# Local attention units at fixed places, turning transfers on two queues, and a later weight split

## The chip, the cores and the metric

One core of one Trainium2 chip runs the kernel. The metric is the device time of one execution in microseconds (us), the median of several runs. TensorE (PE) multiplies; ScalarE (ACT) and VectorE (DVE) work on what it leaves in its accumulators (PSUM banks); GpSimd (POOL) clears tiles and issues transfers; SyncE (SP) only issues transfers (DMA).

## What is computed

Two layers of an encoder over 512 tokens of width 1024. Layer 0 mixes tokens by attention in three head groups (dilations 1, 4 and 16), layer 1 by a gated linear attention. After each mixer comes a SwiGLU.

```python
for g, (window, dilation) in enumerate(((128, 1), (512, 4), (2048, 16))):
    q = rope(rms_norm(qkv[:, :, g, 0], q_gain[g]), positions)
    k = rope(rms_norm(qkv[:, :, g, 1], k_gain[g]), positions)
    o, lse = dilated_window_attention(q, k, qkv[:, :, g, 2], window, dilation)
    outs.append(o); lses.append(lse)
alpha = jax.nn.softmax(jnp.stack(lses, axis=0), axis=0)
out = jnp.sum(alpha[..., None] * jnp.stack(outs, axis=0), axis=0)
h = h + out.reshape(bsz, seq, A_WIDTH) @ w_out
h = h + (jax.nn.silu(g) * u) @ w_down      # g, u = split(rms_norm(h) @ w_gate_up)
```

## The kernel before

Every float32 weight of 128x1024 is split into a high part (`wh`, an ACT copy, L96) and a low part (`wl`, a DVE subtraction, L97), and every product is three matmuls: high by high, low by high, high by low. Weights are loaded through SP's queue (L103), two ahead.

**Attention.** Layer 0 comes in two stages. In each, the work goes by four units u of four heads.

- `attend_dilated(u)` (dilations 4 and 16) projects k, v and q of the unit (`qk_chunk`, `v_chunk`), then computes scores (L777, L782), softmax, transposes and the weighted sum of values. Results go through DRAM (`o_dram`, `st_dram`) by POOL's queue (L765, L793).
- `attend_local(u)` (dilation 1) computes scores (L816) with q and k from `qk_chunk("qk", u)`, the softmax over four pairs of blocks, the transposes (L683), the weighted sum (L723), transposes back (L744), and merges the three groups (`combine`).

A chunk (`chunk_of`, L592 to L594) is 96 matmuls of 128x512 into four PSUM banks (tag "pp", of which there are four), so the next chunk's first matmul waits until ACT has copied the bank out (L614, `zs<-ppp`). After a q or k chunk, ACT and DVE normalize and rotate; DVE transposes blocks of 32 (L636); then **the turning**: 16 transfers of 64 KB (L640, `zq<-zs` or `zs<-zs`), all on SP's queue, carry the blocks to their places; and ACT copies them straight (L649, `zq<-zs` or `qk<-zq`), which the scores read.

**The softmax** (L670 to L675) of one group of scores is a DVE reduction with the mask, an exponential on ACT, and in local units two memsets on POOL of what the mask leaves out (`sm<-`, 64 columns). PE's transposes read the whole tile `sm`. The weighted sum of a group is issued after the next group's transposes (`pending`, `later`).

**The order.** A scheduler of the tile framework places instructions on each engine's queue; a program order, priorities (`high_priority`) and `issue_after` steer it. In `attention`, before, unit u of the local attention is written after the projection of unit u+1, and the scheduler spreads the softmax groups among the matmuls of the chunk that follows. `out_attention` (after the attention phase, called through `swiglu`) multiplies by the output weights in two parts: part 0 with the first half of the heads' outputs, part 1 with the second. `load_h` loads the residual (`h<-in_xT_dram`).

**Gate and up** (`gate_up`) runs six blocks j of columns through seven products each, fed by `forms`; the last block has 256 columns. Sums of weights are formed by transfers that add (POOL, L256). `copy` (L398) takes two accumulators into `g` on ACT. `forms.first` loads the next block's first weights into `wf` and splits them (`ready`) ahead of time.

## Time and profile before

| what | value |
|---|---|
| time, median of 3 runs | 1460.18 us (1459.81 to 1460.34) |
| the profiled execution | 1461.01 us, span 1459.2 us |
| granted TensorE clock, mean | 0.999 |
| local attention stage, from the span's start | about 380 to 545 us |
| last gate and up block of layer 0, of layer 1 | about 753 us, about 1310 us |

Rows of the timeline give the start in us from the span's start, the duration in us, engine, line and operation, output and input, a count where several are grouped, and in brackets the idle time of the engine before it and what released it. Matmuls are pipelined, so one row's duration is longer than the distance to the next. A row of the waits gives the engine, its instruction and what it waited for, with the total in us, the number of times and the longest.

### The profile page before, as it was taken

To read this page: it belongs to the slowest core of one execution; us is meant where nothing else is said; L and a number is where in the kernel's file an instruction comes from. 1 tells how busy PE (TensorE), PEld (TensorE's weight loads), DVE (VectorE), ACT (ScalarE), POOL (GpSimd) and SP (SyncE) were. 2 spreads that over 40 slices of the span, in tenths; PEclk is the share of its full clock that TensorE was granted. 3 is DMA by queue.
4 is the path that set the end of the run, shared out by engine and by line. 5 is a ranking of instruction groups with operands and counts; after the bars stand their busy time and mean duration, and the time that the engine had idled before them with its cause. 6 is when DMAs were issued, how large, how long until landed. Compare 5 with 4: busy or idle time off the path is not lost.

```text
span 1459.2 us, 21024 instructions
## 1 busy us (share of the span) xinstructions
PE 1441.3 (99%) x7742; PEld 1186.7 (81%) x7742; DVE 1012.9 (69%) x1824; ACT 752.6 (52%) x1291; POOL 149.0 (10%) x256
## 2 busy tenths in 40 slices
PE   8999999999999999999999999999999999999998
PEld 6887878787778878888888887888888888879887
DVE  6596867778577769977787334847576987779321
ACT  6344444545566746655566233556744755556221
POOL 0001020100100011122221000000010222221000
PEclk9999999999999999999999999999999999999999
DMA  8644343453533355788777333212156787778431
GB/s 276 180 141 107 102 115 119 109 173 101 136 88 88 104 156 157 215 228 231 231 209 217 98 101 97 89 58 80 52 155 192 214 218 221 217 186 251 144 105 62
DMA packets 99832, 219.62 MB, mean 151 GB/s; under 512 B 15216, under 2 KB 42416, under 8 KB 99728
## 3 DMA queue, kind: packets, MB, share of 16 engines
q1 hardware_dynamic: 83376, 166.74, 35.5%
q0 software_dynamic: 16352, 51.53, 16.1%
q8 instruction: 61, 1.00, 0.3%
q14 instruction: 43, 0.35, 0.1%
HBM read 185.64 MB, written 19.99 MB: 141 GB/s over the span
## 4 chain that ended last, share of the span: by engine, by line
PE 78%; DVE 11%; ACT 4%; DMA 3%; issue 2%; SPq 1%; DVEq 0%; ACTq 0%
PE ppp L110 18%; PE ppp L333 12%; PE ppp L112 9%; PE ppp L592 6%; PE ppp L593 6%; PE ppp L594 6%; PE ppp L338 6%; PE ps L333 4%; DVE wl L97 2%; PE ps L338 2%; PE po L723 2%; DMA wf<-in_gate_up_last_dram 1%; PE ps L683 1%; DVE zs L636 1%; DVE sq L635 1%
## 5 line engine op out<-in xcount | busy, mean ns | idle before, releaser
L97 DVE TENSOR_TENSOR wl<-wf,wh 128x1024 fp32r<-128x1024 f32 (+1 forms) x200 | 239.1, 1196 | 200.8 <-ACT wh L96 200.4
L96 ACT ACTIVATE wh<-wf 128x1024 fp32r<-128x1024 f32 (+1 forms) x200 | 208.4, 1042 | 316.4 <-PE ppp L110 172.7
L592 PE MATMUL ppp<-wh,xs 128*128 128x512 f32 (+1 forms) x672 | 258.5, 386 | 6.8 <-ACT wh L96 5.5
L593 PE MATMUL ppp<-wl,xs 128*128 128x512 f32 (+1 forms) x672 | 257.9, 384 | 0.1
L594 PE MATMUL ppp<-wh,xs 128*128 128x512 f32 (+1 forms) x672 | 257.4, 383 | 0.0
L110 PE MATMUL ppp<-xs,wh 128*128 128x512 f32 x544 | 170.3, 393 | 0.0
L592 PEld LDWEIGHTS ppp<-wh,xs 128*128 128x128 f32 x672 | 127.1, 189 | 35.8 <-ACT wh L96 5.5
L594 PEld LDWEIGHTS ppp<-wh,xs 128*128 128x128 f32 x672 | 127.2, 189 | 25.5 <-issue 1.2
L593 PEld LDWEIGHTS ppp<-wl,xs 128*128 128x128 f32 x672 | 127.2, 189 | 25.0 <-issue 1.1
L96 ACT ACTIVATE wh<-wA 128x1024 fp32r<-128x1024 f32 x88 | 93.4, 1061 | 104.4 <-PE ppp L333 39.5
L333 PE MATMUL ppp<-wh,a 128*128 128x512 f32 (+1 forms) x576 | 139.7, 373 | 1.7 <-ACT g L398 1.7
L97 DVE TENSOR_TENSOR wl<-wA,wh 128x1024 fp32r<-128x1024 f32 x88 | 107.1, 1217 | 20.1 <-ACT wh L96 20.1
L333 PEld LDWEIGHTS ppp<-wh,a 128*128 128x128 f32 x576 | 101.9, 188 | 23.1 <-ACT g L398 4.6
L110 PEld LDWEIGHTS ppp<-xs,wh 128*128 128x128 f32 x544 | 101.7, 188 | 22.5 <-issue 0.8
L112 PE MATMUL ppp<-xs,wl 128*128 128x512 f32 x272 | 106.1, 391 | 0.0
L671 ACT ACTIVATE sm<-sm,st 128x160 f32<-128x160 f32 (+2 forms) x128 | 56.8, 446 | 44.5 <-DVE st L670 44.4
L338 PE MATMUL ppp<-wl,a 128*128 128x512 f32 (+1 forms) x288 | 78.4, 371 | 0.0
L256 POOL DMA_DIRECT2D wA<-in_gate_up_dram x44 | 38.5, 875 | 323.0 <-DVE wl L97 250.9
L333 PE MATMUL ppp<-wh,sh 128*128 128x512 f32 (+1 forms) x192 | 70.3, 371 | 0.0
L333 PE MATMUL ppp<-wh,sl 128*128 128x512 f32 (+1 forms) x192 | 70.3, 371 | 0.0
L333 PE MATMUL ps<-wh,sh 128*128 128x512 f32 (+1 forms) x192 | 70.3, 371 | 0.0
L333 PE MATMUL ps<-wh,sl 128*128 128x512 f32 (+1 forms) x192 | 70.3, 371 | 0.0
(302 smaller groups left out, 2583.0 us busy)
## 6 DMA issues: line engine op xcount, KB each, us to landing
wA<-in_gate_up_dram POOLq DMA_DIRECT2D x52, 512.0 KB, 6.2
wf<-in_gate_up_dram SPq DMA_DIRECT2D x40, 512.0 KB, 5.0
wf<-in_down_dram SPq DMA_DIRECT2D x32, 512.0 KB, 3.7
wf<-in_a_w_v_dram SPq DMA_DIRECT2D x20, 512.0 KB, 3.8
turned<-g POOLq DMA_DIRECT2D x80, 128.0 KB, 7.3
wf<-in_a_w_q_dram SPq DMA_DIRECT2D x16, 512.0 KB, 3.8
zq<-zs SPq DMA_DIRECT2D x128, 64.0 KB, 2.1
wf<-in_a_w_qk_dram SPq DMA_DIRECT2D x16, 512.0 KB, 3.7
```

The source lines that it names most:

```text
L96: nc.scalar.activation(hi, src, AF.Copy)
L97: self.low = nc.vector.tensor_sub(lo, src, hi.bitcast(F32))
L110: mm(out, lhsT=wh, rhs=part, start=start and k + n == 0, stop=False)
L112: self.multiplied = mm(out, lhsT=wl, rhs=x[0], start=False, stop=stop and k == len(w) - 1)
L256: self.added = nc.gpsimd.dma_start(raw[tag][i], dram[block, i], accum_op=ALU.add)
L333: mm(acc[i][:, 0:width], lhsT=x_part[:, i * P:(i + 1) * P], rhs=wh[:, f], start=first, stop=False, skip_group_check=True)
L338: self.multiplied = mm(acc[i][:, 0:width], lhsT=x[k][0][:, i * P:(i + 1) * P], rhs=wl[:, f], start=False, stop=k == last, skip_group_check ...
L592: mm(a, lhsT=xh, rhs=wh[:, f], start=k == 0, stop=False)
L593: mm(a, lhsT=xh, rhs=wl[:, f], start=False, stop=False)
L594: self.multiplied = mm(a, lhsT=xl, rhs=wh[:, f], start=False, stop=k == KT - 1)
L671: nc.scalar.activation(sm[:, w], sm[:, w], AF.Exp, bias=n, scale=-1.0, accum_out=l)
L723: self.nc.tensor.matmul(o, lhsT=vals(i0 + b, c, c0 + a * HD), rhs=pts[a][b][c], start=c == 0, stop=c == 1)
```

## The change

Three things, and what they need.

1. **Turning on two queues.** Of the 16 transfers of each turning, those with a + b odd are issued by GpSimd instead of SP.
2. **Fixed places.** `attend_local` becomes a generator that stops after each softmax group. `chunk_of` and `project` count ticks, one for each block k of a chunk (12 matmuls of 128x512 or 128x256) or of a `project`, and at given ticks a visit runs the next part of a unit, behind the matmul just issued. The 16 visits are spread by hand over qk chunks 2 and 3, two value chunks and part 0 of the output projection, which moves into the attention phase as `out_part(0)`. `load_h` and the splits of the outputs come before it. In `softmax`, the memsets are written ahead of the reduction and the exponential.
3. **A later split.** In the last gate and up block, the splits of `first` are ordered after ACT's copy that was issued last (`issue_after(self.copied.ins)`).

The lines of the changed kernel have other numbers: L640 becomes L652, L614 L625, L616 L627, L649 L661, L670 to L675 L682 to L687, L683 L695, L701 L713, L723 L735, L738 L750, L816 L829, L96 L98, L398 L401.

**ACT, between the last scores of unit 0 and the chunk of unit 3.** `sm` are the exponentials, `pt` and `ob` copies of transposes and of the weighted sum, `zq` the straight copies of unit 1, `zs` the copies that free the chunk's banks. Before:

```order
L671 ACTIVATE sm_4119,st_695_4066<-sm_4119,st_695_4066 128x192
L835 ACTIVATE mw_4459<-mw_4459 128x16
L701 ACTIVATE pt_4163<-ps_4108 128x512
L701 ACTIVATE pt_4165<-ps_4107 128x512
L96 ACTIVATE wh_4664<-wf_4662 128x1024
L649 ACTIVATE zq_3970<-zs_3953 128x512 x4
L614 ACTIVATE zs_4291<-ppp_4167 128x512
L614 ACTIVATE zs_4291<-ppp_4168 128x512
L616 ACTIVATE wb_4294<-zs_4291 128x512
L616 ACTIVATE wb_4299<-zs_4291 128x512
```

And after the change:

```order
L687 ACTIVATE sm_4173,st_708_4160<-sm_4173,st_708_4160 128x256
L713 ACTIVATE pt_4221<-ps_4162 128x512
L713 ACTIVATE pt_4223<-ps_4161 128x512
L661 ACTIVATE zq_3970<-zs_3953 128x512 x4
L750 ACTIVATE ob_4219<-po_4145 128x512
L687 ACTIVATE sm_4231,st_708_4160<-sm_4231,st_708_4160 128x256
L687 ACTIVATE sm_4231,st_708_4160<-sm_4231,st_708_4160 128x192
L687 ACTIVATE sm_4237,st_708_4160<-sm_4237,st_708_4160 128x256
L687 ACTIVATE sm_4237,st_708_4160<-sm_4237,st_708_4160 128x192
L625 ACTIVATE zs_4249<-ppp_3998 128x512
L625 ACTIVATE zs_4249<-ppp_3999 128x512
```

The copies of `zq` were followed at once by those that free the banks (`zs`); now an `ob` and the four exponentials of unit 0's last group stand between them.

**ACT, the last gate and up block of layer 0.** `g_7438` are the two copies of accumulators, `wf` the loaded weights, `a` and `xs` other splits. Before:

```order
L398 ACTIVATE g_7438<-ppp_7195 128x512
L96 ACTIVATE wh_7506<-wf_7504 128x1024
L398 ACTIVATE g_7438<-ppp_7196 128x512
L96 ACTIVATE a_7441<-h_6627 128x512
L96 ACTIVATE xs_7445<-h_6670 128x512
L487 ACTIVATE wA_7773<-h_6716 128x512
L96 ACTIVATE wh_7550<-wf_7548 128x1024
```

And after the change:

```order
L401 ACTIVATE g_7438<-ppp_7195 128x512
L401 ACTIVATE g_7438<-ppp_7196 128x512
L98 ACTIVATE a_7441<-h_6627 128x512
L98 ACTIVATE xs_7445<-h_6670 128x512
L98 ACTIVATE wh_7506<-wf_7504 128x1024
L98 ACTIVATE wh_7550<-wf_7548 128x1024
```

The split of `wf_7504` stood between the two copies; now it stands behind them and behind two other splits, with the split of `wf_7548` next to it.

**POOL, the memsets of units 0 and 1.** `stn` and `on` are loads of what the dilated units left in DRAM. Before:

```order
L675 MEMSET sm_4113 128x64
L675 MEMSET sm_4119 128x64
L673 MEMSET sm_4387 128x64
L800 DMA stn_4928<-st_dram_2574 128x4x8
L803 DMA on_4378<-o_dram_0_1710 128x4x128
L673 MEMSET sm_4393 128x64
L675 MEMSET sm_4434 128x64
```

And after the change:

```order
L684 MEMSET sm_4083 128x64
L682 MEMSET sm_4167 128x64
L652 DMA zs_3953<-zs_3920 32x4x128 x8
L682 MEMSET sm_4173 128x64
L684 MEMSET sm_4231 128x64
L684 MEMSET sm_4237 128x64
L682 MEMSET sm_4421 128x64
L682 MEMSET sm_4427 128x64
```

Eight issues of the turning of unit 1 (`zs_3953`) now stand between two memsets of one softmax group of unit 0 (`sm_4167` and `sm_4173`).

On PE, the matmuls of a chunk between a group's scores and its transposes were 38, 33, 30, 13, 10, 38, 20, 10 and 10 in the first units; after the change they are 42, 32, 16, 21, 43 and 17 full-width ones in the first groups, 33 to 47 half-width ones in the value chunks, and 18 full-width ones in the output projection.

The diff, in full:

```diff
@@ -1,6 +1,7 @@
 import math
-from contextlib import ExitStack, contextmanager
+from contextlib import ExitStack, contextmanager, nullcontext
 from functools import partial
+from itertools import chain
 
 import numpy as np
 
@@ -47,6 +48,7 @@
         self.ps = ctx.enter_context(tc.tile_pool(name="ps", bufs=1, space=PSUM))
         self.dr = ctx.enter_context(tc.tile_pool(name="dr", bufs=1, space=DRAM))
         self.n = 0
+        self.visiting({})
 
     BASE = {"xs": 16, "h": 8, "wf": 2, "wh": 3, "wl": 3, "R": 1, "acc": 1, "sq": 1,
             "cols": 1, "ident": 1, "ones": 1, "eps": 1}
@@ -278,7 +280,8 @@
                 load(0, "wA")
                 return ready("wA")
             load(0, "wf")
-            return ready("wf")
+            with nullcontext() if ahead else self.tc.issue_after(self.copied.ins):
+                return ready("wf")
 
         def second():
             if own and not started:
@@ -575,7 +578,17 @@
             self.mm3(ps, [(wh[:, c], wl[:, c])], [self.x[k]], k == 0, k == KT - 1)
         return ps
 
-    def chunk_of(self, dram, lhs, width=S, ready=None, visit=None):
+    def tick(self):
+        self.ticks += 1
+        visit = self.visits.pop(self.ticks, None)
+        if visit:
+            with self.tc.issue_after(self.multiplied.ins):
+                visit()
+
+    def visiting(self, visits):
+        self.ticks, self.visits = 0, dict(visits)
+
+    def chunk_of(self, dram, lhs, width=S, ready=None):
         nc = self.nc
         acc = [self.p("pp") for _ in range(NT)]
         per = 1024 // width
@@ -592,9 +605,7 @@
                     mm(a, lhsT=xh, rhs=wh[:, f], start=k == 0, stop=False)
                     mm(a, lhsT=xh, rhs=wl[:, f], start=False, stop=False)
                     self.multiplied = mm(a, lhsT=xl, rhs=wh[:, f], start=False, stop=k == KT - 1)
-                if k == 1 and visit:
-                    with self.tc.issue_after(self.multiplied.ins):
-                        visit()
+                    self.tick()
         return acc
 
     def tokens(self, off):
@@ -637,8 +648,9 @@
         turned = self.t("zs" if kind == "qk" else "zq", (P, 4, 4, NT, 32))
         for a in range(4):
             for b in range(4):
-                nc.sync.dma_start(turned[32 * b:32 * b + 32, :, a].rearrange("p c i j -> p c (i j)"),
-                                  blocks[32 * a:32 * a + 32, :, b].rearrange("p c i j -> p c (i j)"))
+                queue = (nc.sync, nc.gpsimd)[(a + b) % 2]
+                queue.dma_start(turned[32 * b:32 * b + 32, :, a].rearrange("p c i j -> p c (i j)"),
+                                blocks[32 * a:32 * a + 32, :, b].rearrange("p c i j -> p c (i j)"))
         if kind == "k":
             return turned
         straight = []
@@ -666,13 +678,13 @@
         sm = self.t("sm")
         for b, (lo, hi) in enumerate(spans):
             w = slice(b * width + lo, b * width + hi)
-            n, l = stats[b]
-            nc.vector.tensor_tensor_reduce(sm[:, w], ps[:, w], mask[:, lo:hi], 1.0, 3e38, ALU.add, ALU.min, n)
-            nc.scalar.activation(sm[:, w], sm[:, w], AF.Exp, bias=n, scale=-1.0, accum_out=l)
             if lo > 0:
                 nc.gpsimd.memset(sm[:, b * width:b * width + lo], 0.0)
             if hi < width:
                 nc.gpsimd.memset(sm[:, b * width + hi:(b + 1) * width], 0.0)
+            n, l = stats[b]
+            nc.vector.tensor_tensor_reduce(sm[:, w], ps[:, w], mask[:, lo:hi], 1.0, 3e38, ALU.add, ALU.min, n)
+            nc.scalar.activation(sm[:, w], sm[:, w], AF.Exp, bias=n, scale=-1.0, accum_out=l)
         return sm
 
     def turned(self, pss, sms, count, width, finish):
@@ -794,8 +806,9 @@
                                 st[32 * r:32 * r + 32].rearrange("p a b c -> p (a b c)"))
         return o_dram, std
 
-    def attend_local(self, u, q, k, v, o_dram, std):
-        nc = self.nc
+    def attend_local(self, u, qk, v, o_dram, std):
+        nc = self.nc
+        q, k = qk[u]
         far = self.t("stn", (P, NT, 2, 4))
         nc.gpsimd.dma_start(far, std.rearrange("(j i a b) -> i j a b", i=P, a=2, b=4))
         for pr in range(2):
@@ -818,11 +831,13 @@
                 for a in range(2):
                     stats = [[st[:, s, i0 + b, a:a + 1] for s in range(2)] for b in range(2)]
                     sms.append(self.softmax(pss[a], spans, 256, self.masks[:, 160:416], stats))
+                yield
                 pts = self.turned(pss, sms, 4, P, self.finish_local)
                 c0 = (u if u < 2 else 0) * 256 + pr * P
-                vals = lambda i, c, f: v[(i + c) % 4][:, f:f + HD]
+                vals = lambda i, c, f: v[u][(i + c) % 4][:, f:f + HD]
                 then = partial(self.turn_back, partial(self.combine, u, pr, far, st, on)) if i0 == 2 else None
                 self.pending = pts, vals, c0, i0, then
+        yield
 
     def combine(self, u, pr, far, st, on, po):
         nc = self.nc
@@ -892,38 +907,48 @@
             v = [self.v_chunk(self.ins["a_w_v0"], 8)] * 2
             self.o = []
             self.inputs_read = False
-            for u in range(4):
-                if u < 3:
-                    qk.append(self.qk_chunk("qk", u + 1))
-                if u > 1:
-                    v.append(self.v_chunk(self.ins["a_w_v0b"][u - 2], 8, 256))
-                if u == 3:
-                    self.o = [self.split(e, (P, S), "xs", "xs") for e in self.o]
-                    self.inputs_read = True
-                self.attend_local(u, *qk[u], v[u], *far[u])
+            qk.append(self.qk_chunk("qk", 1))
+            units = chain.from_iterable(self.attend_local(u, qk, v, *far[u]) for u in range(4))
+            visit = partial(next, units, None)
+            both = lambda: (visit(), visit())
+            visit()
+            self.visiting({n: visit for n in (10, 24, 30)})
+            qk.append(self.qk_chunk("qk", 2))
+            self.visiting({n: visit for n in (4, 8, 20, 28)})
+            qk.append(self.qk_chunk("qk", 3))
+            self.visiting({4: visit, 16: both, 30: visit})
+            v.append(self.v_chunk(self.ins["a_w_v0b"][0], 8, 256))
+            self.visiting({n: visit for n in (12, 28)})
+            v.append(self.v_chunk(self.ins["a_w_v0b"][1], 8, 256))
+            self.load_h(self.ins["xT"], None)
+            self.o = [self.split(e, (P, S), "xs", "xs") for e in self.o]
+            self.inputs_read = True
+            self.visiting({4: both, 10: visit, 16: visit, 22: visit, 28: visit})
+            self.out_part(0)
+            for _ in units:
+                pass
             while self.pending or self.later:
                 self.run_later()
                 self.weigh_pending()
-            self.load_h(self.ins["xT"], None)
 
     def project(self, m, w, c0, xs):
         ps = self.p("pp")
         for k, x in enumerate(xs):
             c = slice((c0 + k) * P, (c0 + k + 1) * P)
             self.mm3(ps, [(w[0][:, c], w[1][:, c])], [x], k == 0, k == len(xs) - 1)
+            self.tick()
         self.nc.vector.tensor_add(self.h[m], ps, self.h[m])
 
-    def out_attention(self):
+    def out_part(self, part):
         half = KT // 2
-        for part in range(2):
-            for t in range(half):
-                w = self.weight(self.ins["a_w_out"][part, t], 1024)
-                for i, m in enumerate((half + t, t)):
-                    self.project(m, w, half * i, self.o[half * part:half * (part + 1)])
-                    if part:
-                        self.enter_blocks(m)
+        for t in range(half):
+            w = self.weight(self.ins["a_w_out"][part, t], 1024)
+            for i, m in enumerate((half + t, t)):
+                self.project(m, w, half * i, self.o[half * part:half * (part + 1)])
                 if part:
-                    self.pair_sums(t)
+                    self.enter_blocks(m)
+            if part:
+                self.pair_sums(t)
 
     def out_gla(self):
         for m in range(KT // 2):
@@ -988,7 +1013,8 @@
         o = [None] * 8
 
         def vals(half, visit):
-            acc = self.chunk_of(self.ins["b_w_v"][half], lambda kk, i: [x[:, i * P:(i + 1) * P] for x in self.x[kk]], visit=visit)
+            self.visiting({2 * NT: visit})
+            acc = self.chunk_of(self.ins["b_w_v"][half], lambda kk, i: [x[:, i * P:(i + 1) * P] for x in self.x[kk]])
             for i in range(NT):
                 vt = self.t("v")
                 ACT(vt, acc[i], AF.Copy, scale=Rc[:, i:i + 1])
@@ -1249,7 +1275,7 @@
             k.attention()
         if "ffn0" in phases:
             assert "attn" in phases
-            k.swiglu(0, 8 if "gla" in phases else None, k.out_attention)
+            k.swiglu(0, 8 if "gla" in phases else None, partial(k.out_part, 1))
         if "gla" in phases:
             if "ffn0" not in phases:
                 k.load_h(ins["xT"], 8)
```

## The prediction

> **What bounds the kernel now.** I read the page first. TensorE (PE) is busy for nearly the whole span, and no other engine comes close.
>
> ```profile
> span 1459.2 us, 21024 instructions
> PE 1441.3 (99%) x7742; PEld 1186.7 (81%) x7742; DVE 1012.9 (69%) x1824; ACT 752.6 (52%) x1291; POOL 149.0 (10%) x256
> ```
>
> So only time in which TensorE stands still can be won. The view of the waits, for PE over the whole span, gives us in total, times, and the longest. The first row is the kernel's start, which the change leaves alone.
>
> ```profile
> PE ppp L592 <- ACT wh L96: 5.5, 1, 5.5
> PE ps L816 <- ACT zq L649: 2.7, 1, 2.7
> PE ppp L333 <- ACT g L398: 1.7, 2, 0.9
> PE ps L683 <- ACT sm L671: 1.3, 5, 0.3
> PE ppp L592 <- ACT zs L614: 1.3, 3, 0.7
> ```
>
> The second row is the largest that the change can touch. Its place, in PE's timeline:
>
> ```profile
> 422.33 0.40 PE L594 MATMUL ppp<-wh,xs 128*128 128x512 f32 x1
> 425.44 1.06 PE L816 MATMUL ps<-zq 64*128 64x192 f32 x8 [2.71 <-ACT zq L649]
> 426.44 0.79 PE L592 MATMUL ppp<-wh,xs 128*128 128x512 f32 x1
> ...
> 429.59 0.47 PE L593 MATMUL ppp<-wl,xs 128*128 128x512 f32 x1
> 429.89 0.40 PE L594 MATMUL ppp<-wh,xs 128*128 128x512 f32 x1
> ```
>
> Matmuls shown as 0.39 us start 0.22 to 0.23 us apart; I count 0.227. The scores of unit 1 could have started at 422.33 + 0.23 = 422.56; they start 2.9 us later. After that the clock is halved: from 426.44 to 429.89 eight matmuls take 3.45 us instead of 8 x 0.227 = 1.82, which is 1.6 us more. The table by windows (us; busy of PE, PEld, DVE, ACT, POOL; granted clock) shows the same:
>
> ```profile
> 425.00:429.00 4.00, 3.56 (x14) 2.71 (x15) 2.35 (x7) 4.00 (x9) 0.00 (x0) 0.66 0.43 135
> ```
>
> This stop costs 2.9 + 1.6 = 4.5 us. What released it, on SP's queue and on ScalarE (ACT):
>
> ```profile
> 410.06 10.27 SPq L640 DMA_DIRECT2D zs<-zs  x16
> 422.77 1.06 ACT L96 ACTIVATE wh<-wf 128x1024 fp32r<-128x1024 f32 x1 [3.34 <-PE ppp L594]
> 423.73 2.17 ACT L649 ACTIVATE zq<-zs 128x512 f32<-128x512 f32 x4
> 425.81 1.06 ACT L614 ACTIVATE zs<-ppp 128x512 f32<-128x512 f32 x2
> ```
>
> Sixteen issues of 0.64 us, then the copies, then the scores.
>
> **Gate and up: -2.0 us.** The last block of each layer, in PE's and ACT's timelines:
>
> ```profile
> 751.16 0.62 PE L338 MATMUL ppp<-wl,sh 128*128 128x512 f32 x2
> ...
> 752.52 0.61 PE L338 MATMUL ppp<-wl,a 128*128 128x512 f32 x2
> 753.94 1.20 PE L333 MATMUL ppp<-wh,a 128*128 128x512 f32 x4 [0.81 <-ACT g L398]
> 752.34 1.06 ACT L96 ACTIVATE wh<-wf 128x1024 fp32r<-128x1024 f32 x1 [1.30 <-DMA wf<-in_gate_up_last_dram]
> 753.31 0.58 ACT L398 ACTIVATE g<-ppp 128x512 f32<-128x512 f32 x1
> 1310.88 1.20 PE L333 MATMUL ppp<-wh,a 128*128 128x512 f32 x4 [0.88 <-ACT g L398]
> ```
>
> PE wants the bank at 752.52 + 2 x 0.227 = 752.97 and gets it 0.97 us later, because the split stands before the second copy and waits for its load. The bank to be copied is complete with the first row, at about 751.8; ordered ahead of the split, the copy (0.6) is done by 752.5, in time. Layer two has the same picture (idle 0.88 by the row, about 1.0 by the pitch). The split itself now follows the copy and two halves of other splits (0.6 each), and ends at about 754.7 (752.5 + 1.2 + 1.06); PE reads it with its half-width matmuls:
>
> ```profile
> 758.15 1.12 PE L333 MATMUL ppp<-wh,a 128*128 128x256 f32 x8
> ```
>
> Some 3 us of matmuls hide its new place; without them its 1.06 us would show. Both stalls go: 0.97 + 1.0 = 2.0, or 1.7 by the sum in the waits.
>
> **Local units, waits before the transposes: -2.0 us.** PE transposes the softmax (L683). In the later units of before, only 8 to 13 full matmuls of 0.227 us (1.8 to 3.0 us) stand between scores and transposes. The chain that must fit is four reductions on VectorE (DVE) and four exponentials with their reads on ACT, which overlap. The groups of the stretch from 375 to 545 us (busy and mean ns, then the idle time before):
>
> ```profile
> L670 DVE CUSTOM_DVE_ANT_0 sm<-ps,masks 128x256 f32<-128x256 f32 x32 | 13.3, 416 | 6.7 <-PE ps L816 6.7
> L671 ACT ACTIVATE sm<-sm,st 128x192 f32<-128x192 f32 x32 | 14.3, 446 | 13.8 <-DVE st L670 13.8
> L614 ACT ACTIVATE zs<-ppp 128x512 f32<-128x512 f32 x12 | 6.7, 591 | 1.6 <-PE ppp L594 1.5
> L738 ACT ACTIVATE ob<-po 128x512 f32<-128x512 f32 x8 | 4.8, 596 | 3.3 <-PE po L723 3.3
> L683 PE MATMUL ps<-ident,sm 128*128 128x128 f32 x128 | 17.1, 276 | 1.9 <-ACT sm L671 1.3
> ```
>
> Here is one unit: DVE's first reduction and ACT's last exponential.
>
> ```profile
> 415.09 0.42 DVE L670 CUSTOM_DVE_ANT_0 sm<-ps,masks 128x256 f32<-128x256 f32 x1 [0.95 <-PE ps L816]
> 417.00 0.44 ACT L671 ACTIVATE sm<-sm,st 128x192 f32<-128x192 f32 x1
> 417.34 0.19 ACT L671 ACTIVATION_READ_ACCUMULATOR sm<-sm,st 128x1 f32 x1
> ```
>
> From 415.09 to 417.53 it takes 2.45 us. The change leaves at least 16 full matmuls (3.6 us) or as long a stretch of half-width ones, so this wait goes everywhere: 1.9 us by the group, and about ten starts late by 0.2 us more than a usual change of shape, 2.0. I take 2.0.
>
> **The turning on two queues.** Eight issues remain on each, about 8 x 0.64 = 5.1 us instead of 10.3. GpSimd (POOL) has issued transfers of this size; its row and the landing medians (KB each, us to landing):
>
> ```profile
> 399.30 2.56 POOL L765 DMA_DIRECT2D o_dram<-ob  x4 [28.28 <-DVE ob L762]
> zq<-zs SPq DMA_DIRECT2D x128, 64.0 KB, 2.1
> o_dram<-ob POOLq DMA_DIRECT2D x32, 64.0 KB, 3.0
> ```
>
> So POOL's issue is 0.64 us too, and the landing 0.9 us later: a turn is done 5.1 - 0.9 = 4.2 us sooner. The Trainium skill ("DMA: Bandwidth & Descriptors", Anatomy of one DMA - SWDGE (gpsimd) path) fits a GpSimd transfer at 2.0 us plus bytes over 436e3, about 2.15 us here as an estimate, which would make it 5.1; the row says 3.0, and I go by the row.
>
> With unit 1's turning 4.2 us earlier and its scores 24 rows further back in the order of PE, its old stop of 4.5 us goes. But a wait takes its place. In the new order ACT has, between the last scores of unit 0 and the copy (L614's, zs_4249) that frees the bank for the first matmul of the chunk of unit 3, the copies of zq, one ob, four exponentials and then that copy. PE has 6 matmuls there, 1.4 us. After the scores the softmax takes 2.45 us, the copy 0.59: 3.0 - 1.4 = 1.6 us at the least. If the turned data land later than the scores, 2.17 of copies and 0.60 of ob stand ahead as well; by my addition of the rows from the end of unit 1's chunk that is up to 3.0. I take 1.7. The same pattern stands before the first matmul of the next value chunk (zs_4633): 12 matmuls, 2.7 us of cover, against 2.45 + 2.17 + 0.59 = 5.2 if all the copies come between, 3.0 if they are done in time; 0.3 to 2.5, I take 1.5.
>
> POOL also zeroes the unused part of sm before each masked exponential, and the transposes wait for that. In the new order two memsets (sm_4173, sm_4980) stand right behind eight turning issues, 5.1 us of queue; one ends about when PE wants it. No row shows such a wait; between nothing and 1.2 in all (two issues of 0.6), I take 0.5. Loading the tokens' residual earlier and the earlier splits of o stand on SP, ACT and DVE beside matmuls: nothing, for DVE and ACT are free for a third and half of the span; uncovered, one such copy of 512 columns would show its 0.6 us.
>
> **Dilated units: +0.3.** There the scheduler places each unit's scores 27 matmuls (6.1 us) earlier, 35 (7.9) in the last. In before, the last copies and the scores of the first and the last unit:
>
> ```profile
> 106.80 1.15 ACT L649 ACTIVATE qk<-zq 128x512 f32<-128x512 f32 x2 [4.09 <-DMA zq<-zs]
> 110.38 0.49 PE L777 MATMUL ps<-zq,qk 64*128 64x128 f32 x4
> ...
> 343.91 1.15 ACT L649 ACTIVATE qk<-zq 128x512 f32<-128x512 f32 x2 [7.44 <-DMA zq<-zs]
> 346.62 0.49 PE L777 MATMUL ps<-zq,qk 64*128 64x128 f32 x4
> ```
>
> The copies ended at 107.95, 2.4 us ahead. 6.1 - 2.4 = 3.7 is needed and 4.2 gained. That holds with 0.5 to spare. In the last unit 7.9 - 1.6 = 6.3 is needed; there the order has DVE's part of the turning some 3 us earlier too, so 4.2 + 3 is enough. I take 0.3 for small waits, 0 to 2.
>
> **Sum.** Removed: 4.5 + 2.0 + 2.0 = 8.5. New: 1.7 + 1.5 + 0.5 + 0.3 = 4.0. Net -4.5. The profiled execution took 1461.0 us, 0.8 above the median of 1460.2; 1461.0 - 4.5 - 0.8 = 1455.7. With the new costs at their ends (1.9 to 6.5) it goes from 1453.6 to 1458.2. A measurement of this kernel tells 0.2%, 2.9 us, from no change: below 1457.3 is faster.
>
> **Rivals.**
> *A, no new wait:* the copies that free the banks come in time and the whole 8.5 is won: 1461.0 - 8.5 - 0.8 = 1451.7. For it: ACT is idle half the time, and the addition of rows over 30 us may be off by the 2 us in question. Against it: the softmax of 2.45 us can't be hidden by 1.4 us of matmuls.
> *B, the new wait halves the clock as the old one did:* the zs_4249 wait is 3.0 and 1.6 behind it, the value chunk 2.1, memsets 1.0, dilated 0.3: 8.0, net -0.5, 1459.7 after the same 0.8. For it: a gap of 2.9 us did it at 425 us. Against it: the gaps of about 1 us at 752.97 and 1309.8 did not; matmuls follow there at full pitch. The Trainium skill ("TensorE: Matmul & The Clock Gate", What's actually happening) halves the clock after an idle window of about 3.4 us that runs free of the kernel; here 2.9 was enough, so the row decides, and by the page gaps of 1.7 would cost nothing more.
> *C, slower:* GpSimd's half of the turning lands too late in the dilated units. If its issues take 0.88 us, as its adding loads of weights do, eight take 7.0, and with 0.9 of landing a turn is only 2.4 sooner:
>
> ```profile
> L256 POOL DMA_DIRECT2D wA<-in_gate_up_dram x44 | 38.5, 875 | 323.0 <-DVE wl L97 250.9
> ```
>
> Then three units wait 3.7 - 2.4 = 1.3 each, the last 6.3 - 2.4 = 3.9 (without DVE's earlier part) with 1.6 of half clock: 9.4, and -4.5 turns into +4.9, 1465.1. It decides from a turn less than 3.7 us shorter. For it: POOL's queue also holds stores that wait for DVE. Against: the 64 KB row, 0.64.
> *That the change doesn't do what it says* can't be for the order, which shows it.
>
> **Chances.** The forecast 0.45 (0.36 of it below 1457.3), A 0.20, B 0.20, C 0.15. Faster 0.36 + 0.20 + 0.02 of B = 0.58; same 0.09 + 0.18 = 0.27; slower 0.15. The range takes in A with a little of its own spread, 1450.5, and reaches into C, 1462.5, leaving out some 0.15.
>
> **What would show it.** No idle on the second g copy near 751 and 1307 us; none before the scores of unit 1; no full clock lost there; turning rows of eight on SPq and eight on POOL, each about 5.1 us; an idle of 1 to 3 us on a 128x512 matmul released by ACT's zs right after unit 0's last scores, and one at the start of the first value chunk. Wrong: waits of the dilated scores for DMA (C), or none on zs at all (A).

## The result, and the profile after

| what | before | after |
|---|---|---|
| time, median (range) of 5 runs | 1460.18 us (1459.81 to 1460.50) | 1466.04 us (1464.89 to 1467.74) |
| the profiled execution, its span | 1461.01, 1459.2 us | 1465.28, 1463.5 us |
| granted TensorE clock, mean | 0.999 | 0.997 |

The ratio is 1.0038, with an interval of 1.0027 to 1.0048: slower by 5.9 us by the medians, by 4.3 in the two profiled executions. The forecast was 1455.7, and its range ended at 1462.5, so it was wrong in sign and in size. (One correction to the section on the change: a tick is three matmuls, one block of tokens of one k, not twelve.)

The busy times on the page after, and PE's waits over the whole span:

```profile
PE 1443.3 (99%) x7742; PEld 1193.2 (82%) x7742; DVE 1013.5 (69%) x1824; ACT 752.7 (51%) x1291; POOL 201.0 (14%) x352
```

```profile
PE ppp L605 <- ACT zs L625: 7.1, 5, 3.5
PE ppp L605 <- ACT wh L98: 5.4, 1, 5.4
PE ppp L112 <- ACT v L673: 1.3, 1, 1.3
```

The waits for ACT's copy of `zq` (2.7) and of `g` (1.7) are gone; waits for banks (`zs`, 7.1) stand in their place. That would be about a draw. But PE's busy time has grown too, from 1441.3 to 1443.3 with the same 7742 matmuls: part of the loss is inside rows that count as busy. So I took the distance from each matmul's start to the next, in both traces, and summed by stage what exceeds a pitch of its shape, the same in both (0.227 us for 128x512, 0.120 for 128x256, 0.104 for the 64x128 of the dilated scores, and so on). The stages are cut at 90 and 375 us, and at the first matmuls of gate and up and of the linear attention:

| stage | before, us | after, us | difference |
|---|---|---|---|
| start | 2.40 | 1.77 | -0.63 |
| dilated units | 14.48 | 19.93 | +5.45 |
| local units, output projection | 9.56 | 10.70 | +1.14 |
| gate and up, down, layer 0 | 2.31 | 1.95 | -0.36 |
| linear attention | 7.76 | 7.84 | +0.08 |
| gate and up, down, layer 1 | 2.19 | 0.87 | -1.32 |

These sum to the +4.4 by which PE's first start and last start lie further apart. Most of the loss is in the dilated units, the stage for which the prediction had 0.3.

**The dilated units.** PE's timeline at the scores of unit 2, before and then after:

```profile
265.83 0.49 PE L777 MATMUL ps<-zq,qk 64*128 64x128 f32 x4
266.26 0.29 PE L782 MATMUL ps<-zq,zq 64*32 64x32 f32 x16
266.48 0.49 PE L777 MATMUL ps<-zq,qk 64*128 64x128 f32 x4
266.90 0.29 PE L782 MATMUL ps<-zq,zq 64*32 64x32 f32 x16
267.12 0.50 PE L592 MATMUL ppp<-wh,xs 128*128 128x512 f32 x1
```

```profile
260.57 0.88 PE L789 MATMUL ps<-zq,qk 64*128 64x128 f32 x4
261.38 0.85 PE L794 MATMUL ps<-zq,zq 64*32 64x32 f32 x16
262.16 0.49 PE L789 MATMUL ps<-zq,qk 64*128 64x128 f32 x4
262.58 0.29 PE L794 MATMUL ps<-zq,zq 64*32 64x32 f32 x16
262.80 0.50 PE L605 MATMUL ppp<-wh,xs 128*128 128x512 f32 x1
```

The same 40 small matmuls take 267.12 - 265.83 = 1.29 us before and 262.80 - 260.57 = 2.23 after, with no idle time in brackets: the first half is stretched (0.81 and 0.78 instead of 0.43 and 0.22), the second is as before. Before, all sixteen such blocks take 1.29. After, the first block of each unit takes 2.23, 1.89, 2.23 and 2.59, and the second 1.45, 1.55, 1.55 and 1.29; the rest 1.29. That is 4.46 us of the 5.45. The first blocks stand where the turned data have just arrived. The copies that straighten them, on ACT, before and after:

```profile
262.30 1.15 ACT L649 ACTIVATE qk<-zq 128x512 f32<-128x512 f32 x2 [4.13 <-DMA zq<-zs]
```

```profile
259.89 1.15 ACT L661 ACTIVATE qk<-zq 128x512 f32<-128x512 f32 x2 [0.98 <-DMA zq<-zs]
```

Before, they end at 263.45, 2.4 us ahead of the scores. After, the second ends at 261.04, 0.5 us behind the scores' start. But the first block reads, of the two, only the first copy (`q1[pr]` with `pr` 0), which was done at 260.53, and turned tiles that had landed by 259.32 (the chain below). So its data are there when it starts at 260.57, and what stretches it is not a wait for them. The last unit, in PE's timeline and by the table of windows, also loses a wait of 1.07 and some clock:

```profile
341.29 0.88 PE L789 MATMUL ps<-zq,qk 64*128 64x128 f32 x4 [1.07 <-ACT qk L661]
342.10 0.91 PE L794 MATMUL ps<-zq,zq 64*32 64x32 f32 x16
```

```profile
344.00:347.00 3.00, 3.00 (x8) 2.41 (x9) 2.88 (x15) 1.76 (x8) 0.00 (x0) 0.59 0.00 0
```

A granted clock of 0.59 instead of 1.0 over 3 us costs 1.2. With 4.5 for the blocks and 1.2 for the wait (by the pitch) that makes 6.9; about 1.4 comes back in small differences of either sign elsewhere in the stage.

**How long a turning takes.** The queues of SP, before and after, and of POOL after, at unit 2:

```profile
250.51 10.25 SPq L640 DMA_DIRECT2D zq<-zs  x16
```

```profile
251.26 5.80 SPq L652 DMA_DIRECT2D zq<-zs  x8
251.78 4.34 POOL L652 DMA_DIRECT2D zq<-zs  x8 [39.40 <-DVE zs L647]
```

From the first issue to the straight copies it took 262.30 - 250.51 = 11.8 us before and 259.89 - 251.26 = 8.6 after: 3.2 sooner, where the prediction had 4.2. Why, the landing medians after (KB each, us to landing) and a piece of the chain that ended last (start, us, what) show:

```profile
zq<-zs SPq DMA_DIRECT2D x64, 64.0 KB, 3.2
zq<-zs POOLq DMA_DIRECT2D x64, 64.0 KB, 2.9
```

```profile
256.21 3.12 DMA zq<-zs
259.32 0.02 issue
259.35 0.04 ACTq L661
...
259.89 0.64 ACT qk L661
260.53 0.04 issue
260.57 0.88 PE ps L789 x4
```

SP's own transfers, 2.1 us to landing before, take 3.2 when both queues issue (1.0 lost); SP's eight issues take 5.80 instead of 8 x 0.64 = 5.1 (0.7 more, of which some 0.5 falls before the last issue); and ACT passes seven semaphores one after the other, 259.32 to 259.89, before it copies (0.6; before, its copy started 0.07 behind the last landing). Together about 2.1 of the 5.1 us saved: 3.0, near the 3.2 seen. POOL's half was not the late one: it issued its eight in 4.34 us.

**The local units.** PE's and ACT's timelines after, at the banks:

```profile
426.33 0.50 PE L605 MATMUL ppp<-wh,xs 128*128 128x512 f32 x1 [2.83 <-ACT zs L625]
462.70 0.58 PE L605 MATMUL ppp<-wh,xs 128*128 128x256 f32 x1 [3.49 <-ACT zs L625]
507.40 0.74 PE L112 MATMUL ppp<-xs,wh 128*128 128x512 f32 x2 [1.29 <-ACT v L673]
```

```profile
421.27 2.19 ACT L661 ACTIVATE zq<-zs 128x512 f32<-128x512 f32 x4 [0.65 <-DMA zs<-zs]
423.37 0.58 ACT L750 ACTIVATE ob<-po 128x512 f32<-128x512 f32 x1
423.84 0.50 ACT L687 ACTIVATE sm<-sm,st 128x256 f32<-128x256 f32 x1
...
425.70 1.06 ACT L625 ACTIVATE zs<-ppp 128x512 f32<-128x512 f32 x2
```

The stop before unit 1's scores is gone. In its place PE stands 3.0 us (by the pitch) at the chunk of unit 3, because the copy that frees its bank is behind `zq`, `ob` and four exponentials; 3.65 at the first value chunk; and 1.45 at the output projection, for a copy of values. Behind the second of them the clock is halved, as the table by windows shows (granted clock third from the end):

```profile
462.00:467.00 5.00, 4.30 (x24) 4.31 (x25) 3.57 (x8) 5.00 (x11) 0.00 (x0) 0.66 0.00 0
```

From 462.70 to 466.01 half-width matmuls start 0.21 us apart instead of 0.12, 1.5 us in all. So 3.0 + 3.65 + 1.5 + 1.45 = 9.6 us are new, against 4.5 for the old stop and about 3.3 for the transposes' waits that went. That would leave 1.8, where the table has 1.14; 0.7 comes back in small differences that I did not follow one by one.

**Gate and up.** ACT's timeline after, layer 0:

```profile
756.48 0.60 ACT L401 ACTIVATE g<-ppp 128x512 f32<-128x512 f32 x1 [1.20 <-PE ppp L341]
757.84 0.60 ACT L401 ACTIVATE g<-ppp 128x512 f32<-128x512 f32 x1 [0.76 <-PE ppp L341]
```

The second copy waits only for its matmuls, and PE does not stop there.

### The profile page after: what moved, and what is told of

Same layout as the page of the kernel before. It is cut to its first block, busy times and chain, and to the rows that moved or that the text cites. A ratio compares the mean times of both kernels' runs of the same rounds, so it can differ in the third digit from the quotient of the medians.

```text
span 1463.5 us, 21179 instructions
## 1 busy us (share of the span) xinstructions
PE 1443.3 (99%) x7742; PEld 1193.2 (82%) x7742; DVE 1013.5 (69%) x1824; ACT 752.7 (51%) x1291; POOL 201.0 (14%) x352
## 4 chain that ended last, share of the span: by engine, by line
PE 84%; DVE 8%; ACT 3%; DMA 2%; issue 1%; SPq 1%; DVEq 0%; ACTq 0%
PE ppp L112 19%; PE ppp L336 13%; PE ppp L114 9%; PE ppp L605 7%; PE ppp L607 7%; PE ppp L606 7%; PE ppp L341 6%; PE ps L336 5%; PE ps L341 2%; PE po L735 2%; DVE wl L99 2%; PE ps L789 1%; PE ps L695 1%; SPq L652 1%; DVE sq L644 1%
## 5 line engine op out<-in xcount | busy, mean ns | idle before, releaser
L98 ACT ACTIVATE wh<-wf 128x1024 fp32r<-128x1024 f32 (+1 forms) x200 | 208.4, 1042 | 326.8 <-PE ppp L112 175.5
L98 ACT ACTIVATE wh<-wA 128x1024 fp32r<-128x1024 f32 x88 | 93.3, 1061 | 101.7 <-PE ppp L336 38.8
L687 ACT ACTIVATE sm<-sm,st 128x160 f32<-128x160 f32 (+2 forms) x128 | 56.9, 446 | 63.3 <-DVE st L686 63.3
```

The lines of the kernel that those rows point to most:

```text
L98: nc.scalar.activation(hi, src, AF.Copy)
L687: nc.scalar.activation(sm[:, w], sm[:, w], AF.Exp, bias=n, scale=-1.0, accum_out=l)
```

## Experiments

After the result I held theory W: PE has to pass more semaphores ahead of the scores when two queues wrote what they read (the score lines of one unit wait for a transfer 24 times before, 32 times after), and each costs time. Its rivals were P, the fixed places cost (the earlier scores, whatever the queue), and L, the turned data are simply late through the slower queue. Later came S: the number of checks does not matter by itself; they are free while PE's sequencer runs ahead of the matmuls, and cost about 0.12 us each once it is held at the first of them, as it is when the scores stand where their data just land. All ratios are to before, run beside it on the same chip. Runs 1 to 4, 5 to 8 and 9 to 11 were on one chip each, so across these groups the ratios are compared, not the times.

**1. Both queues, without fixed places or the later split** (before, changed):

```diff
-                nc.sync.dma_start(turned[32 * b:32 * b + 32, :, a]...,
+                queue = (nc.sync, nc.gpsimd)[(a + b) % 2]
+                queue.dma_start(turned[32 * b:32 * b + 32, :, a]...,
```

> The kernel before with one part of the change: every second turning transfer on GpSimd's queue, everywhere. Theory W (the cost of the change lies in the dilated scores: TensorE reads the turned tiles themselves there, so with two kinds of queues it has to check sixteen semaphores instead of eight, one after another, between score matmuls of 30 ns): the first score block of each dilated unit takes 1.9 to 2.6 us instead of 1.29, the stage is about 5 us longer, unit 1's stop before its local scores (4.5 us) shrinks by up to 4; in all 1461 to 1466. Rival P (the fixed places of the local units cost the time, the queues do not): the dilated blocks stay at 1.29 and the time falls by 2 to 4, about 1457.

Measured: 1463.75 us, 1.0021 (1.0011 to 1.0031). The first blocks take 2.15, 1.84, 1.84 and 2.29; there is a wait of 1.47 and half clock at unit 3; the dilated stage has 19.7 us of excess (14.5 before), the local one 8.3 (9.6 before). The two queues alone bring nearly the whole loss of the dilated units, 5.2 of 5.45, since the scheduler then places the scores earlier by itself. P falls for that stage.

**2. Dilated turnings all on GpSimd, local ones on SP** (before, changed: `queue = nc.sync if kind == "qk" else nc.gpsimd`).

> The kernel before, with all sixteen transfers of the k and q turnings of the dilated units on GpSimd's queue; the local units' stay on SP's. One kind of queue, but the slow one. Theory W: as many semaphores as before, so the score blocks stay near 1.3 us and the dilated stage within 1 us of before: 1459 to 1462. Rival L (GpSimd's transfers arrive late, and that is what stretches the score blocks): all of a score's data come this way now, so the blocks are at least as long as in the changed kernel (1.9 to 2.6) and the time 1465 or more.

Measured: 1462.83, 1.0009 (1.0000 to 1.0019). All blocks take 1.29 but the last unit's first, 1.93. One queue, slow or not, brings no loss in the other units: L falls, in the form that the slower queue as such stretches the blocks. At this point W seemed to hold; the last unit's block comes back under run 9.

**3. After, with the dilated turnings on SP only:**

```diff
-                queue = (nc.sync, nc.gpsimd)[(a + b) % 2]
+                queue = (nc.sync, nc.gpsimd)[(a + b) % 2 if kind == "qk" else 0]
```

> The changed kernel, with the k and q turnings of the dilated units back on SP's queue alone; the local units' turnings stay on both queues. Theories W and L: the dilated stage is as before, -5.9 us against the changed kernel, the local stage as in it: about 1460. Rival P: the dilated part does not matter, and the time stays at 1464 to 1466.

Measured: 1461.97, 1.0002 (0.9993 to 1.0011); all blocks 1.29. Undoing the second queue in the dilated units takes 3.6 per mille, 5 us, off the changed kernel. The local waits remain (2.95 and 3.69, both with half clock behind them, and 1.45).

**4. As 3, with the visits at earlier ticks:**

```diff
-            self.visiting({n: visit for n in (10, 24, 30)})
+            self.visiting({n: visit for n in (6, 16, 26)})
...
-            self.visiting({n: visit for n in (4, 8, 20, 28)})
+            self.visiting({n: visit for n in (4, 8, 16, 24)})
...
-            self.visiting({n: visit for n in (12, 28)})
+            self.visiting({n: visit for n in (10, 22)})
```

> As the run with the dilated turnings on SP, and the visits moved away from the ends of the chunks: ticks (6, 16, 26), (4, 8, 16, 24) and, for the second value chunk, (10, 22) in place of (10, 24, 30), (4, 8, 20, 28) and (12, 28). If the waits of 3.0, 3.7 and 1.5 us at the starts of the next chunks come from ACT's order (straight copies and four exponentials between the last scores and the copies that free the banks), scores 20 to 26 matmuls ahead of the chunk's end hide most of them: 5 to 8 us less than the run with the dilated turnings on SP, 1452 to 1455. If they come from the turned data's landing, they stay, within 1.5 us of that run.

Measured: 1460.51, 0.9988 (0.9977 to 0.9999). A gain of 1.5 us on run 3, far less than expected. The waits are 1.55 at 422.8 and 3.17 at 458.9 (a clock of 0.50 over the 2 us behind it), and the third is gone. The second stayed, and ACT's timeline there says why:

```profile
456.20 2.19 ACT L661 ACTIVATE zq<-zs 128x512 f32<-128x512 f32 x4 [2.57 <-DMA wf<-in_a_w_v0b_dram]
458.29 1.06 ACT L625 ACTIVATE zs<-ppp 128x512 f32<-128x512 f32 x2
```

The copy that frees the bank is not behind the softmax any more but behind the straight copies, which wait 2.57 us with ACT idle (the row names a transfer of SP's queue; the turning of the same chunk is what they read). An earlier softmax could not move it.

**5. Only the k turnings on GpSimd, q on SP** (before, changed: `queue = nc.gpsimd if kind == "k" else nc.sync`). The scores read k and q, so both queues are waited for as in the changed kernel, but neither is shared within one turning.

> The kernel before, with only the k turnings of the dilated units on GpSimd's queue (all sixteen transfers); q and the local units stay on SP's. The k data land tens of us before any score reads them. Theory W (the count of semaphores that TensorE checks between score matmuls): k and q now have eight each, sixteen in all, so the first score block of each unit takes 1.8 to 2.6 us and the time is 1463 to 1465. Rival M (it is one tile's halves coming by two queues, or their late arrival, that stretches the blocks): every tile comes by one queue and in time, so the blocks stay at 1.29 us and the time at 1460 to 1461.

Measured: 1461.03, 0.9998 (0.9988 to 1.0008); all blocks 1.29. PE's timeline at unit 2:

```profile
266.24 0.49 PE L778 MATMUL ps<-zq,qk 64*128 64x128 f32 x4
...
267.52 0.50 PE L592 MATMUL ppp<-wh,xs 128*128 128x512 f32 x1
```

Two queues are read and nothing is lost. But the run does not test W's count: the expectation took the waits to rise, and the trace has 24 on transfers in a unit's score lines, as before. Only run 9 decides that. The trace also shows PE's checks for these scores, all but the last two, at 262.1 to 265.3, under the matmuls ahead of them. From this I formed S.

**6. The later split alone** (before, with the `issue_after(self.copied.ins)` of the change).

> The kernel before with the later split of the last gate and up block alone. If the stop of 1.0 us in each layer was ACT's order, as predicted, both go and nothing comes: -2.0 us, 1458.5 to 1459. If the time is given back behind it (the split or its load late), -0.5 or less.

Measured: 1460.10, 0.9993 (0.9985 to 1.0002): 1.0 us, and the interval takes in none. Both stops are gone, and 0.33 and 0.25 us of new ones stand at 786 and 797 us. The time alone doesn't tell 2.0 from 0.5; the stops do tell that the split works.

**7. As 4, with the straight copies of units 1 and 2 ordered behind the next chunk's four bank copies:**

```diff
+        if kind == "qk" and u > 1:
+            with self.tc.issue_after(freed.ins):
+                self.straighten()
...
-            nc.scalar.activation(e.rearrange("p (i a j) -> p i a j", i=NT, a=4), ...)
...
+        if kind == "qk" and u in (1, 2):
+            self.straighten = straighten
+        else:
+            straighten()
```

> As the run with the visits moved, and ACT's straight copies of units 1 and 2 ordered behind the four copies that free the next chunk's banks. If the waits left at the starts of the chunks (1.6 and 3.2 us) come from straight copies that wait for the turning, with the copies that free the banks behind them, both go and the half clock behind them: 4 to 6 us less than that run, 1454.5 to 1456.5. If the banks are held up by the exponentials alone, less than 1.5 us.

Measured: 1458.18, 0.9978 (0.9969 to 0.9987). It beats both kernels; but by the ratios it is 1.0 per mille, 1.5 us, better than run 4, where 4 to 6 were expected. The waits are 0.44 at 421, 2.07 at 456 and 1.08 at 500. What is left at 456, on ACT and on PE:

```profile
455.41 1.09 ACT L625 ACTIVATE zs<-ppp 128x512 f32<-128x512 f32 x2 [4.22 <-DMA wf<-in_a_w_v0b_dram]
```

```profile
456.06 0.39 PE L605 MATMUL ppp<-wh,xs 128*128 128x256 f32 x1 [1.91 <-ACT zs L625]
```

Now the first bank copy itself waits, ACT idle for 4.22 us: it writes a `zs`, of which there are two, and the turning before still reads one. That is my inference from the two buffers; run 10 bears on it.

**8. As 7, with every turning on SP.**

> As the run with the deferred straight copies, with every turning back on SP's queue alone. If the second queue's shorter turning (4 us) is what the local units need, unit 1's or unit 2's scores wait again for it: 2 to 5 us more than that run. If the deferred copies leave room for the whole turning, the same within 1 us.

Measured: 1461.86, 1.0004 (0.9995 to 1.0013): 3.7 us slower than run 7, with waits of 3.39 at 423.9 (and half clock) and 1.79 at 460.4. In the local units the second queue is worth its price.

**9. After, with both queues everywhere, but each unit's dilated scores held back to about their old place:**

```diff
+        def rest():
+            for pr in range(2):
...
+        self.visiting({53 if u < 3 else 57: rest})
```

(The body of `rest` is the scores and what follows them, unchanged.)

> The changed kernel, all its turnings on two queues, with the first scores of each dilated unit held back to the place that they had before the change (a visit at tick 53 behind the next unit's first matmul, 57 for the last unit; without it they stand 27 to 35 matmuls earlier). TensorE has exactly the changed kernel's waits on semaphores in those scores, 32 to a unit instead of 24. Theory W, in the form that the count of waits between the scores costs the time: the first blocks stay at 1.9 to 2.6 us and the time at 1464 to 1466. Theory S (the scores stand where the last data only just land, so that TensorE's sequencer is held at the first wait, loses its lead, and pays every wait behind it in the open): the blocks go back to 1.29, the waits pass ahead under the matmuls, and the time falls by 4 to 6, to 1460 to 1462.

Measured: 1461.77, 1.0003 (0.9993 to 1.0014), where the changed kernel had 1.0038. The same transfers, the same semaphores, nearly the same landing medians (3.1 and 3.0, after 3.2 and 2.9). At unit 2, ACT's copies and PE's scores:

```profile
258.19 1.16 ACT L661 ACTIVATE qk<-zq 128x512 f32<-128x512 f32 x2 [0.76 <-DMA zq<-zs]
```

```profile
265.11 0.49 PE L792 MATMUL ps<-zq,qk 64*128 64x128 f32 x4
...
266.39 0.50 PE L605 MATMUL ppp<-wh,xs 128*128 128x512 f32 x1
```

The data are there at 259.35, 5.8 us ahead, and the block takes 1.28 again; every unit's first block is 1.3. Later ones are not all so: two take 1.42 and 1.55, and one of the last unit, placed in two halves, 2.4 in all. The stage's excess is 15.2, 0.7 above before and 4.8 below the changed kernel. The count of separate semaphore instructions on PE's weight queue, with the first and last start, of before, after and this run in turn, shows that none went away (the second score line has 32 in all three):

```profile
L777 PEldq EVENT_SEMAPHORE  x19: 51/51/51, 106.2 to 344.7; - x19
```

```profile
L789 PEldq EVENT_SEMAPHORE  x35: 51/51/51, 98.9 to 341.6; - x35
```

```profile
L792 PEldq EVENT_SEMAPHORE  x35: 51/51/51, 105.7 to 342.4; - x35
```

Unit 2 has 17 of them, in the changed kernel and in this run. Here fifteen start between 260.96 and 264.13, the last five 0.45 us apart, under the 512-wide matmuls ahead of the scores at 265.11; two stand at 265.13 and 265.25, and the scores are not longer for them. In the changed kernel five pass early, the sixth is held until 260.57, and with it twelve start about 0.12 us apart up to 261.90, among the score matmuls. (The second blocks hold none of them. Their 0.68 of the 4.46 us is another matter: there the weight loads wait for ACT's copies of transposes, six times and 1.3 us in all in these lines, where before it was twice and 0.5.) The exception of run 2 shows the same with the 24 waits of before. ACT's copies and PE's first block in its last unit:

```profile
345.85 1.15 ACT L650 ACTIVATE qk<-zq 128x512 f32<-128x512 f32 x2 [2.36 <-DMA zq<-zs]
```

```profile
346.62 0.58 PE L778 MATMUL ps<-zq,qk 64*128 64x128 f32 x4
347.13 0.85 PE L783 MATMUL ps<-zq,zq 64*32 64x32 f32 x16
```

The first copy ends just ahead of the block, and ten checks start about 0.12 us apart from 346.53 to 347.65, while the block takes 1.93 us. So S is shown: the same checks cost nothing in one place and lengthen the block in the other, and 24 waits in the bad place lengthen it where 32 in the good one do not.

**10. As 7, with nine of sixteen local transfers on GpSimd and the value chunk's visits at 6 and 16** instead of 10 and 22.

> As the run with the deferred straight copies, with nine of a local turning's sixteen transfers on GpSimd's queue (which takes 0.54 us for each against SP's 0.8) and the second value chunk's visits at ticks (6, 16) in place of (10, 22). If the 2.1 us left before the first value chunk is the turning's end (its source tile is the buffer that the next copies need), it shrinks by 0.5 to 1; if the 1.1 us before the output projection is four exponentials ahead of the value copies, it goes: 1 to 2 us less, 1456 to 1457. If neither, the same within 0.5.

Measured: 1458.19, 0.9977 (0.9965 to 0.9988), the same as run 7, where 1456 to 1457 were expected. The wait at 456 is down from 2.07 to 0.37 and that at 500 from 1.08 to 0.26. The row of ACT's bank copy now names the turning itself, as run 7's inference had it:

```profile
452.54 1.08 ACT L625 ACTIVATE zs<-ppp 128x512 f32<-128x512 f32 x2 [2.32 <-DMA zs<-zs]
```

But two waits of the transposes for the softmax have come, 0.96 at 466.2 and 1.75 at 491.0. What one place gives another takes.

**11. Before, with the later split and two queues for the local turnings alone**, no fixed places (`(a + b) % 2 if kind == "qk" else 0`).

> The kernel before with the later split and with the local units' turnings alone on two queues; no fixed places, dilated turnings on SP. If the second queue is all that the local units lack, their stop of 4.5 us before unit 1's scores goes to 1 or less and the time is 1455 to 1457; if the loss moves on (to the waits before the transposes, or to the copies that free the banks), 1458 to 1460, and the fixed places are worth their 2 us only together with the deferred copies.

Measured: 1458.81, 0.9980 (0.9970 to 0.9990). Within the interval it is as good as runs 7 and 10. Unit 1's stop is gone; 1.13 at 457.4, 1.53 at 496.3 and 0.64 at 443.4 have come. So the fixed places, even with the deferred copies, won nothing that these measurements can tell from the two queues and the split without them.

## Why the prediction was wrong

**The step that failed is the dilated term:** "3.7 is needed and 4.2 gained. That holds with 0.5 to spare ... I take 0.3 for small waits, 0 to 2." It cost 5.45. Two things in it were wrong. First the gain: the turning came 3.2 us sooner, not 4.2, because landing on SP's queue went from 2.1 to 3.2 us, SP's issues became slower, and ACT has more semaphores to pass. The sum had charged only POOL's half with a longer landing, and took SP's row from a trace in which SP issued alone. Second the price: being half a microsecond late was taken to cost half a microsecond. But PE's checks for each transfer, hidden under wide matmuls before, then come one behind the other among the scores, and a block of 1.29 us becomes 1.9 to 2.6 (run 9). Undoing the queue there (run 3) or holding the scores back (run 9) takes the loss away; both bring the changed kernel down to the time of before.

**Rival C** named this place and its point of decision, a turn less than 3.7 us sooner, and that point was passed (3.2). Its cause was another: not GpSimd's issues, which took 0.54 us each, less than the 0.64 that the sum used, but SP's transfers and the checks. It gave 1465.1 with 9.4 us for the dilated units (and counted their 0.3 besides); they cost 5.45. Near the measured 1466.0 it came only because the local units gave less than it assumed, so its nearness is luck.

**Unit 1's stop (4.5) and the waits before the transposes (2.0)** went as said; the latter were about 3.8 us by the pitch before and 0.5 after.

**New waits for banks (1.7 + 1.5)** were of the right kind and too small: 3.0 and 3.65, for the straight copies came before the bank copies at both, which the text had as its worse end. The clock was halved behind the second for 1.5, which the sum had at neither (rival B had it behind the first, where matmuls run at full pitch). A third wait, 1.45 for the values at the output projection, was not foreseen. Together the local stage came out at +1.1 instead of 1.7 + 1.5 + 0.5 - 4.5 - 2.0 = -2.8.

**POOL's memsets (0.5)** cost nothing that the trace shows: those behind the turning issues of unit 1 start at 418.45 and end at 418.7, ahead of PE's transposes at 418.9.

**Gate and up (-2.0)** gave -1.3 in layer 1 and -0.4 in layer 0, where the stop of 0.97 went, 0.28 at 781 us came and a wait at 602 grew by 0.2; run 6 shows new stops behind the later split as well. Their cause I have not tried to settle.

So of the 8.9 us between -4.5 and the +4.4 in PE's starts, 5.15 are the dilated units, 3.9 the local ones, 0.3 gate and up and 0.1 the linear attention; the start gave 0.6 back. One slip of the sum stands beside that: with all the new costs at their upper ends it is 3.0 + 2.5 + 1.2 + 2 = 8.7 and not 6.5, which would have taken the forecast's own span to 1460.4.

## What to carry to other kernels

When a transfer is split over two queues, count with the landing times of both queues running, and give every reader's new semaphore checks a place under long instructions: data that arrive just in time are late for an engine that has a dozen checks to pass. A faster transfer also moves the consumer, if a scheduler places it, so its old slack is not there to be spent. And before waits are moved by hand, look which of the copies in one engine's queue frees the next bank: here two queues where the transfers were late, with no fixed places at all, won as much (2.0 per mille) as fixed places with the straight copies ordered behind the bank copies (2.2), both with the later split.

## What the runs showed of the hardware

- **Two queues at once.** A 64 KB turning transfer lands in 2.1 us on SP's queue alone, and in 3.1 to 3.6 us on SP's and 2.9 to 3.7 on GpSimd's when both issue (after and runs 1, 3, 9). With all of a dilated turning on GpSimd (run 2) it takes 2.7. With k on GpSimd and q on SP (run 5) q keeps its 2.1, and k takes 3.3. GpSimd's issue took 0.54 us each, and SP's rose from 0.64 to 0.71 to 0.83.
- **Semaphore checks.** Recorded at 51 ns, they follow one another at about 0.12 us on PE's weight queue when nothing covers them, and at some 0.08 us on ACT.
- **The clock.** In the clock records of these traces every halved stretch lasts 3.41 us and begins a whole number of 3.41 us after the clock first rose. Cut into such windows, the traces show when a stop cost clock. Every window in which PE stood still for 2.0 to 3.4 us (by the pitch, in stops of over a quarter of a microsecond) was followed by a halved clock: the stop before unit 1's scores in before, that at 463 in after, and those in runs 2, 3, 4, 8 and 9. None with 1.8 or less was, but for two of 1.2 (after, 341) and 1.0 (run 1), where the stretched scores stand in the same window. The stop of 3.0 at 426 in after fell into two windows, 1.65 and 1.35, and cost no clock. Nor did the old stop of 2.9 in runs 5 and 6, which was cut in the same way; so the 1.6 us that the prediction added for its clock hung on where the stop fell. The Trainium skill ("TensorE: Matmul & The Clock Gate", What's actually happening) has idle windows that run free of the kernel, with which this agrees; its about 3.4 us is longer than most gaps that were enough.
